# FFN down projection in seven products of 512x512 blocks held in PSUM, with the gated rows kept on chip

## The chip, the cores and the metric

The kernel runs on one core of a Trainium2 chip. The metric is the device time of one execution in microseconds (us), lower is better. Engines are named as in the profile: PE (TensorE, matmuls), PEld (its weight loads), DVE (VectorE), ACT (ScalarE), POOL (GpSimd), SP (SyncE, which here only issues transfers). A name with q (SPq, POOLq) is the queue through which an engine issues transfers.

## The reference

Two residual layers over 1024 positions of width 1024 in float32: layer 0 mixes with causal differential attention and pooling, layer 1 with sliding-window attention, and each ends with the same gated feed-forward block. The change is in that block's last product alone.

```python
D_MODEL, SEQ, D_FF, DEPTH = 1024, 1024, 2816, 2

def conv_glu_ffn(x, norm_g, w_up, conv_w, conv_b, w_down):
    h = rms_norm(x, norm_g) @ w_up                       # (S, 2*D_FF)
    hp = jnp.pad(h, ((0, 0), (CONV_W - 1, 0), (0, 0)))
    c = conv_b
    for j in range(CONV_W):
        c = c + conv_w[j] * hp[:, j:j + S]
    gate, up = jnp.split(c, 2, axis=-1)
    return x + (jax.nn.silu(gate) * up) @ w_down         # the down projection

for layer in range(DEPTH):
    x = mixer(layer, x)
    x = conv_glu_ffn(x, ...)
```

## The kernel before

Activations lie transposed, channels on the 128 partitions and positions along the free axis, so x is 8 tiles of 128x1024 and the gated result G of an FFN is NF = 22 row blocks of 128x1024. Every product is made in three matmuls: each operand is split into a high part (fp32r, written by ACT, L127) and a low part (the rest, L128, on DVE or POOL), and hi x hi, hi x lo and lo x hi are added up in a PSUM bank of 128x512 (`mm3`, L114).

The up pass (`ffn_up`, L310) makes G block by block. It already multiplies 512x512 blocks in seven products, with the sums of weight blocks made on DVE (L430) and parts of results saved from PSUM by ACT (`snap`, L456). Its last steps for block 21 are matmuls (L336), bank sums (L460), a convolution over time (ACT L343, DVE L344 and L346), the gate's SiLU (ACT L352), the gated product (DVE L356) and a write of the block to DRAM, to the tile `gd`.

The down pass (`ffn_down`, L511) reads G back. It goes over pairs of row blocks: `fetch` loads two blocks of w_down (SP, into `wr`) and two of G (POOL, L523, into `gr`; the first pair into `xg`), each 512 KB, and splits them at full width (1024 columns) on ACT and DVE. `contract` (L256) then goes over the 16 banks of the output (8 row blocks d, 2 halves h of the positions), makes 6 matmuls in each (L119) and adds the bank to the x tile on DVE (L268). So x in SBUF is read and written 16 times per pair, 11 pairs per pass. For layer 0 the last pair is left to `layer_c` (L1046), which runs its first half, starts the query projection (`project_qk`, matmuls L553) and weaves the second half with it. With the last addition for a block goes `after`: in layer 0 `feed` (L1121) makes the next norm's inputs (ACT L220, L224, DVE L221, L229, then `norm_stats`, PE transposes L236 and a DVE reduction L238), in layer 1 a store to the output (L1184).

Buffers are pools with a number of slots by tag: `ws` 8 (split operands), `wr` 2 (raw weights), `x` 8, `xg` 16 (the split inputs of a projection, 4 KB a partition each), `rbc` 1, and in the down pass `gr` 4 and `g` 8. PSUM has 8 banks in tags s (3), q (3) and d (2). The order on each engine is not the order of the code: a scheduler lays the instructions out by priority on a simulated time line, and `urgent(n)` lifts the priority of what is inside it. Each engine then runs its instructions in that fixed order; one that waits holds up all behind it on its engine, and so do the transfers of one queue.

Of the kernel before, what the change touches and what calls it, by code (L numbers as in the profile page):

```python
# [25 lines left out]
HALF = 512  # L26
NF = 22
# [28 lines left out]
LO_OUT = 0  # L56

# [7 lines left out]
class Trunk:  # L65
# [16 lines left out]
    DOWN = {"gr": 4, "g": 8}  # L82
# [428 lines left out]
    def ffn_down(self, layer, xs, gd, after, begin=lambda: None):  # L511
        nc, I = self.nc, self.I

        def fetch(i):
            ws, gs = [], []
            for k in range(2):
                for lst, tag, stage, src in (
                        (gs, "g", "gr", gd[(i + k) * P:(i + k + 1) * P, :]),
                        (ws, "ws", "wr", I["w_down"][layer, i + k])):
                    if i == 0 and lst is gs:  # L520
                        tag = stage = "xg"
                    raw = self.big(stage)
                    (nc.gpsimd if lst is gs else nc.sync).dma_start(raw[:], src)  # L523
                    hi, lo = self.big(tag, F32R), self.big(tag, F32R)
                    with self.urgent():
                        self.split(raw[:], hi[:], lo[:])
                    lst.append((hi, lo))
            return ws, gs
# [517 lines left out]
    def layer_c(self, w0, norm, before, xd, after):  # L1046
# [27 lines left out]
        x, sp = [], []  # L1074
# [58 lines left out]
    def run(self):  # L1133
# [38 lines left out]
        def begin():  # L1172
            self.norm_begin(2, False)
            w0.extend(self.in_weights(I["c_q"][0]))
# [99 lines left out]
```

## Time and profile before

| what | us |
|---|---|
| median of 3 runs (2156.82 to 2160.39) | 2159.76 |
| the profiled execution | 2160.71 |
| its span, first to last instruction | 2158.9 |
| PE busy in it | 2071.0 |
| DVE busy | 1609.1 |
| ACT busy | 1018.2 |
| POOL busy | 229.1 |
| DMA traffic, mean over the span | 86 GB/s |

The two down passes lie at about 846 to 1120 us and 1899 to 2156 us of the span; the up passes before them take about 410 to 869 and 1455 to 1915 us. Busy times of PE include the overlap of matmuls that follow each other; how far apart they start is read from the timeline. The mean granted clock of the run is 0.985 of full speed.

### The profile page before, as it was taken

What the parts mean: (1) busy time and instruction counts of PE and PEld (TensorE: products, weight loads), DVE (VectorE), ACT (ScalarE), POOL (GpSimd) and SP (SyncE); (2) the same over time, 40 slices, a digit from 0 to 9 for tenths busy, and PEclk for the clock granted to TensorE, in tenths of its full rate; (3) what the DMA queues carried; (4) which work ended last, traced back from release to release, by engine and by line L of the source; (5) the groups of instructions that cost most, each with busy time, mean ns of one, the idle gap of its engine ahead of it and who ended that gap; (6) DMA issues with size and microseconds to landing.
All of it is one profiled execution on the core that took longest, in us unless ns stands there. A gap on an engine that the chain in (4) does not pass through costs nothing.

```text
span 2158.9 us, 28587 instructions
## 1 busy us (share of the span) xinstructions
PE 2071.0 (96%) x10704; PEld 1767.5 (82%) x10704; DVE 1609.1 (75%) x2790; ACT 1018.2 (47%) x1895; POOL 229.1 (11%) x397
## 2 busy tenths in 40 slices
PE   8999999889999999899999999898999999989999
PEld 6999877677888888788899988776788888878887
DVE  6677777887777787766684887777877787776765
ACT  5476755454555555212155776553645445531210
POOL 1331542000000000100023230200000000010000
PEclk9999999999999999999999999999999999999999
DMA  4210221312222213522231111221222212262222
GB/s 167 88 50 21 79 89 57 109 34 94 78 88 88 84 73 104 213 104 86 71 127 42 48 40 40 79 79 40 97 78 88 88 71 86 88 240 82 88 89 78
DMA packets 59611, 186.03 MB, mean 86 GB/s; under 512 B 6864, under 2 KB 7376, under 8 KB 59472
## 3 DMA queue, kind: packets, MB, share of 16 engines
q1 hardware_dynamic: 43920, 140.16, 18.7%
q0 software_dynamic: 8640, 31.46, 4.1%
q10 hardware_dynamic: 6912, 12.59, 1.5%
q8 instruction: 84, 1.38, 0.3%
q14 instruction: 55, 0.45, 0.1%
HBM read 142.23 MB, written 41.94 MB: 85 GB/s over the span
## 4 chain that ended last, share of the span: by engine, by line
PE 87%; DVE 7%; ACT 4%; issue 1%; DMA 0%; POOL 0%; SPq 0%; DVEq 0%; ACTq 0%; POOLq 0%
PE pss L336 23%; PE psq L336 12%; PE psd L119 12%; PE psq L119 11%; PE pss L119 8%; PE psd L553 6%; PE psd L336 5%; PE pss L553 3%; PE psq L726 2%; PE pss L778 1%; PE pss L624 1%; PE pss L625 1%; PE psq L778 1%; DVE x L305 1%; DVE t L1014 1%
## 5 line engine op out<-in xcount | busy, mean ns | idle before, releaser
L336 PE MATMUL pss<-xg,ws 128*128 128x512 f32 x1248 | 298.8, 393 | 15.9 <-DVE xg L128 9.2
L336 PEld LDWEIGHTS pss<-xg,ws 128*128 128x128 f32 x1248 | 235.6, 189 | 68.5 <-DVE xg L128 10.1
L336 PE MATMUL pss<-T,ws 128*128 128x512 f32 x912 | 224.5, 389 | 3.4 <-ACT ws L127 3.4
L119 PE MATMUL psq<-g,ws 128*128 128x512 f32 x852 | 219.1, 391 | 2.5 <-ACT g L127 2.5
L336 PEld LDWEIGHTS pss<-T,ws 128*128 128x128 f32 x912 | 171.0, 188 | 39.7 <-ACT ws L127 4.2
L119 PEld LDWEIGHTS psq<-g,ws 128*128 128x128 f32 x852 | 160.2, 189 | 36.0 <-ACT g L127 3.0
L553 PE MATMUL psd<-ws,xg 128*128 128x256 f32 x1344 | 184.0, 284 | 2.2 <-DVE hms L562 1.7
L119 PE MATMUL psd<-xg,ws 128*128 128x512 f32 x624 | 168.0, 406 | 15.4 <-DVE x L268 14.6
L127 ACT ACTIVATE ws<-wr 128x512 fp32r<-128x512 f32 (+1 forms) x176 | 145.3, 829 | 72.4 <-PE pss L119 36.3
L127 ACT ACTIVATE g<-gr 128x1024 fp32r<-128x1024 f32 x40 | 42.0, 1051 | 290.4 <-PE pss L119 289.4
L119 PE MATMUL pss<-g,ws 128*128 128x512 f32 x684 | 176.2, 391 | 0.0
L553 PEld LDWEIGHTS psd<-ws,xg 128*128 128x128 f32 x1344 | 171.4, 191 | 4.8 <-DVE hms L562 2.5
L336 PE MATMUL psq<-xg,ws 128*128 128x512 f32 x696 | 169.5, 392 | 0.0
L128 DVE TENSOR_TENSOR ws<-hf,ws 128x512 fp32r<-128x512 f32 x152 | 104.0, 688 | 69.1 <-ACT ws L127 68.9
L336 PEld LDWEIGHTS psq<-xg,ws 128*128 128x128 f32 x696 | 131.9, 190 | 27.6
L268 DVE TENSOR_TENSOR x<-psq,x 128x512 f32<-128x512 f32 x160 | 109.6, 687 | 56.8 <-PE psq L119 56.5
L119 PEld LDWEIGHTS pss<-g,ws 128*128 128x128 f32 x684 | 129.3, 189 | 26.9
L119 PEld LDWEIGHTS psd<-xg,ws 128*128 128x128 f32 x624 | 115.1, 193 | 39.6 <-DVE x L268 17.1
L268 DVE TENSOR_TENSOR x<-psd,x 128x512 f32<-128x512 f32 x160 | 109.8, 687 | 47.0 <-PE psd L119 43.3
L128 DVE TENSOR_TENSOR ws<-wr,ws 128x512 fp32r<-128x512 f32 (+1 forms) x138 | 119.3, 865 | 20.6 <-ACT ws L127 20.6
L119 PE MATMUL psd<-g,ws 128*128 128x512 f32 x528 | 134.0, 389 | 0.0
L127 ACT ACTIVATE ws<-hf 128x512 fp32r<-128x512 f32 x152 | 94.9, 629 | 65.4 <-PE psq L336 27.2
(229 smaller groups left out, 3849.2 us busy)
## 6 DMA issues: line engine op xcount, KB each, us to landing
wr<-in_dram SPq DMA_DIRECT2D x130, 512.0 KB, 3.7
gd<-x SPq DMA_DIRECT2D x40, 512.0 KB, 2.6
gr<-gd POOLq DMA_DIRECT2D x40, 512.0 KB, 3.8
x<-in_dram SPq DMA_DIRECT2D x38, 512.0 KB, 4.5
xd<-x ACTq DMA_DIRECT2D x48, 256.0 KB, 2.1
x<-in_dram SPq DMA_DIRECT2D x32, 256.0 KB, 4.0
x<-xd POOLq DMA_DIRECT2D x16, 512.0 KB, 6.7
t<-in_dram SPq DMA_DIRECT2D x10, 512.0 KB, 3.6
```

The source lines that it names most:

```text
L119: self.nc.tensor.matmul(out, a, b, start=(k == 0), stop=(k == n - 1))
L127: nc.scalar.activation(hi, raw, AF.Copy)
L128: (eng or nc.vector).tensor_tensor(out=lo, in0=raw, in1=hi.bitcast(F32), op=ALU.subtract)
L268: nc.vector.tensor_tensor(out=xs, in0=po[:], in1=xs, op=ALU.add)
L305: nc.vector.scalar_tensor_tensor(out=xs, in0=xs, scalar=g, in1=self.nrbc[:, sl], op0=ALU.mult, op1=ALU.mult)
L336: nc.tensor.matmul(bank[:], a, b, start=start and k == 0, stop=k == n - 1, skip_group_check=open)
L553: self.nc.tensor.matmul(out, a, m[:, d % 4, :], start=(n == 0), stop=(n == 23))
L624: nc.tensor.matmul(out, q[:, qs], his[m][:, ks], start=True, stop=False)
L625: nc.tensor.matmul(out, q[rows, qs], lo[rows, ks], start=False, stop=True)
L726: nc.tensor.matmul(po[:, :256], tt[:, kb * P:(kb + 1) * P], v, start=(b == 0 and t == 0), stop=(b == j and t == 1))
L778: nc.tensor.matmul(pu[:], a, b, start=d + n == 0, stop=d == ND - 1 and n == 2)
L1014: nc.vector.tensor_scalar(pv[:, n, k0:2 * P], pv[:, n, k0:2 * P], rl[:, n:n + 1], None, ALU.mult)
```

## The change

`ffn_down` is written anew. The output is four blocks, C = [[C11, C12], [C21, C22]], of 512 channels by 512 positions, the weights four blocks by half of the 22 row blocks and half of the output channels, and G four blocks by half of the row blocks and half of the positions. Seven products of such blocks, instead of eight, give all four, with sums of weight blocks and of G blocks as operands. Each product goes over K = 11 steps; a step makes four banks of 3 matmuls (L610 in the new file), and the four banks stay in PSUM over the whole product, some over several: products 1, 6, 7 and 4 add up in one set of banks, 5 and 3 in another, 2 in a third. After each product its four banks are added to x (L632, 28 times per pass).

G is now loaded once, in halves of 512 columns (POOL queue), into 11 tiles `b` and 11 of the `xg` tiles and stays there; the sums of G blocks are made in place on DVE (L573). The weight sums of products 5, 6 and 3 are kept in 5 more `xg` tiles and the `rbc` tile. Weights come in halves of rows (SP), in tiles that hold two halves; where both belong to two steps, one transfer of 512 KB brings them, elsewhere two of 256 KB. `lead` prepares the operands of step n + 3 (AHEAD) and asks for the weights of step n + 9 (FETCH) at each step. The halves of the first four G blocks are loaded early into `hf` tiles (EARLY). Splits are at 512 columns.

In layer 0 the next norm is begun after product 3 and fed with the first half of the positions after products 3 and 7, with the second after 2 and 4; the first weights of the query projection are loaded after product 2, and `layer_c` runs product 4 whole before it starts that projection in the code.

```diff
@@ class Trunk
-    DOWN = {"gr": 4, "g": 8}
+    DOWN = {"b": 11, "r": 3}
@@ ffn_down
-        nxt = fetch(0)
-        x = [self.big("x") for _ in range(ND)]
-        for d in range(ND):
-            nc.gpsimd.dma_start(x[d][:], xs[d * P:(d + 1) * P, :])
-        for i in range(0, NF - 2, 2):
-            ws, gs = nxt
-            nxt = fetch(i + 2)
-            self.drain(self.contract(ws, [self.halves(g) for g in gs], x, banks="dqsdqsqs"))
-        ws, gs = nxt
-        begin()
-        return lambda h: self.contract(ws, [self.halves(g) for g in gs], x, after, "qd", (h,))
+        K = NF // 2
+        seq = [(p, k) for p in (1, 5, 6, 3, 7, 2, 4) for k in range(K)]
+        pairs = {1: (0, lo), 6: (0, lo), 3: (K, lo), 2: (K, lo), 4: (K, hi)}
+        stages = {p: ("r", "wr", "r", "wr", "r") for p in (5, 6, 3, 7, 2)}
+        stages[1], stages[4] = ("wr", "wr", "r", "r", "r"), ("r",)
...
+        b1 = [self.half() for _ in range(EARLY)]
+        for k in range(EARLY):
+            nc.gpsimd.dma_start(b1[k][:], g(k, hi))
+        bb = [self.big("b") for _ in range(K)]
+        cc = [self.big("xg") for _ in range(K)]
+        b11, b21 = [t[:, lo] for t in bb], [t[:, hi] for t in bb]
+        b12, b22 = [t[:, lo] for t in cc], [t[:, hi] for t in cc]
+        held = [self.big("xg") for _ in range(5)] + [self.big("rbc")]
+        sums = [held[k // 2][:, (k % 2) * HALF:(k % 2 + 1) * HALF] for k in range(K)]
...
+        def prepare(p, k):
+            r = raws.pop((p, k))
+            with self.urgent(9000):
+                if p == 1:
+                    l, m = r, b1[k][:] if k < EARLY else b11[k]
+                elif p == 5:
+                    l = combine(sums[k], r[0], r[1], ALU.add)
+                    m = combine(b11[k], b12[k], b11[k])
+                elif p == 6:
+                    l = combine(sums[k], sums[k], r)
+                    m = combine(b11[k], b22[k], b11[k])
+                elif p == 3:
+                    l, m = combine(sums[k], r, sums[k]), b22[k]
+                elif p == 7:
+                    l = combine(r[0], r[0], r[1])
+                    m = combine(b22[k], b22[k], b12[k])
+                elif p == 2:
+                    l, m = r, b21[k]
+                else:
+                    l, m = r, combine(b21[k], b21[k], b11[k])
+                ops[p, k] = operand(l), operand(m)
...
+        def product(p):
+            if p in (1, 5, 2):
+                banks[p] = [self.bank(t) for t in ("ssqd" if p == 1 else "sqqd")]
+            else:
+                banks[p] = banks[5] if p == 3 else banks[1]
+            n0 = seq.index((p, 0))
+            last = K - 2 if p == 4 else K
+            for k in range(last):
+                for m in range(4):
+                    multiply(p, k, m)
+                lead(n0 + k)
+            for m in range(4):
+                for k in range(last, K):
+                    multiply(p, k, m)
+            d0 = 4 if p in (5, 7, 4) else 0
+            cols = hi if p in (1, 2, 4) else lo
+            for m in range(4):
+                xm = x[d0 + m][:, cols]
+                with self.urgent(12000):
+                    nc.vector.tensor_tensor(out=xm, in0=banks[p][m][:], in1=xm, op=ALU.add)
...
+        for p in (1, 5, 6, 3):
+            product(p)
+        begin(0)
+        done(0, 0)
+        product(7)
+        done(4, 0)
+        after(None, 0, None)
+        product(2)
+        begin(1)
+        done(0, 1)
+        def rest():
+            product(4)
+            done(4, 1)
+            after(None, 1, None)
...
@@ layer_c
-        self.drain(before(0))
+        self.drain(rest)
         q0 = self.project_qk(w0, norm, qs[0], "s", "rbc")
-        ahead = before(1)
-        self.drain(islice(ahead, 4))
-        for _ in ahead:
-            next(q0)
```

Where instructions stand now is told by the built program's order, not by the code. Lines of the new file are 3 higher than before up to `ffn_up`: L336 is now L339, L460 is L463, L344, L346 and L356 are L347, L349 and L359, and the low part of a split, L128, is L131.

DVE at the end of layer 0's up pass, before: the last bank sums (L460), convolutions (L344, L346) and gated product (L356) of block 21 (x_1536 and x_1537), between splits of the down pass (L128) and its first additions of banks to x (L268).

```order
L460 TENSOR_TENSOR x_1535_8139<-snap_1534_8137,psq_1533_8112 128x512
L460 TENSOR_TENSOR x_1530_8076<-snap_1532_8110,psq_1533_8112 128x512
L128 TENSOR_TENSOR ws_1570_8243<-wr_1568_8240,ws_1569_8242 128x1024
L344 SCALAR_TENSOR_TENSOR x_1536_8154<-x_1535_8139,conv_1042_4996,x_1536_8154 128x1023
L344 SCALAR_TENSOR_TENSOR x_1537_8171<-x_1530_8076,conv_1042_4996,x_1537_8171 128x1023
L346 SCALAR_TENSOR_TENSOR x_1536_8154<-x_1535_8139,conv_1042_4996,x_1536_8154 128x1022
L346 SCALAR_TENSOR_TENSOR x_1537_8171<-x_1530_8076,conv_1042_4996,x_1537_8171 128x1022
L128 TENSOR_TENSOR g_1561_8225<-gr_1559_8222,g_1560_8224 128x1024
L268 TENSOR_TENSOR x_1551_8206<-psd_1571_8246,x_1551_8206 128x512
L268 TENSOR_TENSOR x_1551_8206<-psq_1572_8254,x_1551_8206 128x512
L356 TENSOR_TENSOR x_1536_8154<-x_1537_8171,x_1536_8154 128x1024
```

DVE at the same place now; ws_1597 and ws_1598 are the two operands of step 5 of product 1, from the weight tile r_1581 and the G tile b_1547.

```order
L463 TENSOR_TENSOR x_1535_8139<-snap_1534_8137,psq_1533_8112 128x512
L573 TENSOR_TENSOR xg_1565_8212<-wr_1602_8381 128x512
L347 SCALAR_TENSOR_TENSOR x_1536_8154<-x_1535_8139,conv_1042_4996,x_1536_8154 128x1023
L463 TENSOR_TENSOR x_1530_8076<-snap_1532_8110,psq_1533_8112 128x512
L349 SCALAR_TENSOR_TENSOR x_1536_8154<-x_1535_8139,conv_1042_4996,x_1536_8154 128x1022
L347 SCALAR_TENSOR_TENSOR x_1537_8171<-x_1530_8076,conv_1042_4996,x_1537_8171 128x1023
L349 SCALAR_TENSOR_TENSOR x_1537_8171<-x_1530_8076,conv_1042_4996,x_1537_8171 128x1022
L131 TENSOR_TENSOR ws_1597_8342<-r_1581_8282,ws_1597_8342 128x512
L359 TENSOR_TENSOR x_1536_8154<-x_1537_8171,x_1536_8154 128x1024
L131 TENSOR_TENSOR ws_1598_8345<-b_1547_8194,ws_1598_8345 128x512
```

The additions to x that stood here are gone, and an operand of the running product stands behind the gated product instead.

PE around the norm statistics of the first half in layer 0 (transposes into a bank of tag d), before: they stand between matmuls of the query projection (L553) and of the last pair.

```order
L553 MATMUL pss_1904_10052<-ws_1860_9767,xg_1851_9754 128x256
L553 MATMUL pss_1904_10052<-ws_1861_9768,xg_1851_9754 128x256
L553 MATMUL pss_1904_10052<-ws_1860_9767,xg_1852_9755 128x256
L236 MATMUL psd_1878_9882<-idn_122,hf_1863_9781 128x128 x4
L119 MATMUL psd_1889_9921<-g_1812_9592,ws_1815_9598 128x512
L119 MATMUL psd_1889_9921<-g_1813_9593,ws_1815_9598 128x512
```

PE around the same statistics now: the fourth step of product 2 (three banks), the transposes (L239), and then the fourth bank, psd_1785, of the first four steps.

```order
L610 MATMUL pss_1782_9593<-ws_1787_9612,ws_1786_9609 128x512 x2
L610 MATMUL psq_1783_9594<-ws_1787_9612,ws_1786_9609 128x512 x2
L610 MATMUL psq_1784_9595<-ws_1787_9612,ws_1786_9609 128x512 x2
L239 MATMUL psd_1773_9567<-idn_122,hf_1736_9288 128x128 x4
L610 MATMUL psd_1785_9596<-ws_1763_9498,ws_1762_9495 128x512 x3
L610 MATMUL psd_1785_9596<-ws_1765_9516,ws_1764_9513 128x512 x3
L610 MATMUL psd_1785_9596<-ws_1768_9536,ws_1767_9533 128x512 x3
L610 MATMUL psd_1785_9596<-ws_1787_9612,ws_1786_9609 128x512 x3
```

The statistics moved ahead by most of two products, out of the projection and into product 2.

## Rows read from the trace of the kernel before

**Rows 1.** From the page: engines' busy time; chain that ended last, by engine.

```profile
PE 2071.0 (96%) x10704; PEld 1767.5 (82%) x10704; DVE 1609.1 (75%) x2790; ACT 1018.2 (47%) x1895; POOL 229.1 (11%) x397
...
PE 87%; DVE 7%; ACT 4%; issue 1%; DMA 0%; POOL 0%; SPq 0%; DVEq 0%; ACTq 0%; POOLq 0%
```

**Rows 2.** Windows (length, busy per engine, PE clock, DMA share, GB/s): up, starts, steady.

```profile
567.00:594.00 27.00, 27.00 (x121) 22.36 (x120) 22.83 (x30) 13.88 (x20) 0.00 (x0) 1.00 0.16 59
864.00:891.00 27.00, 21.29 (x88) 17.17 (x87) 20.04 (x24) 10.66 (x11) 6.29 (x12) 0.87 0.91 335
918.00:945.00 27.00, 27.00 (x121) 22.36 (x120) 18.98 (x27) 3.91 (x4) 1.06 (x2) 1.00 0.36 123
1917.00:1944.00 27.00, 21.29 (x85) 17.09 (x84) 23.92 (x30) 7.51 (x8) 5.16 (x10) 0.87 0.86 311
```

**Rows 3.** Timeline of PE in the steady pass: start, length, group, count.

```profile
894.11 2.88 PE L119 MATMUL psd<-g,ws 128*128 128x512 f32 x12
896.83 1.52 PE L119 MATMUL psq<-g,ws 128*128 128x512 f32 x6
```

**Rows 4.** Timeline of PE at the first pass's start; in brackets the wait.

```profile
868.97 1.52 PE L119 MATMUL pss<-xg,ws 128*128 128x512 f32 x6
870.33 1.52 PE L119 MATMUL psq<-xg,ws 128*128 128x512 f32 x6
877.57 2.93 PE L119 MATMUL psd<-xg,ws 128*128 128x512 f32 x6 [5.71 <-DVE x L268]
```

**Rows 5.** Window of 5 us behind that wait, columns as in rows 2.

```profile
875.00:880.00 5.00, 2.44 (x6) 1.96 (x7) 5.00 (x7) 3.83 (x4) 2.05 (x4) 0.50 1.02 406
```

**Rows 6.** Timeline of PE at the second pass's start.

```profile
1923.86 2.93 PE L119 MATMUL psd<-xg,ws 128*128 128x512 f32 x6 [5.71 <-DVE x L268]
1926.59 2.45 PE L119 MATMUL psq<-xg,ws 128*128 128x512 f32 x6
```

**Rows 7.** Groups by line and form (busy us, mean ns, idle before): splits, SiLU.

```profile
L128 DVE TENSOR_TENSOR ws<-hf,ws 128x512 fp32r<-128x512 f32 x152 | 104.0, 688 | 69.1 <-ACT ws L127 68.9
...
L127 ACT ACTIVATE ws<-hf 128x512 fp32r<-128x512 f32 x152 | 94.9, 629 | 65.4 <-PE psq L336 27.2 <-ACT ws L127 23.6 <-DVE hf L430 9.0
...
L352 ACT ACTIVATE x<-x 128x1024 f32<-128x1024 f32 x40 | 42.5, 1062 | 46.0 <-DVE x L346 46.0
```

**Rows 8.** Timeline of DVE in the up pass, back to back.

```profile
707.13 0.69 DVE L128 TENSOR_TENSOR ws<-x,ws 128x512 fp32r<-128x512 f32 x1
707.73 0.69 DVE L430 TENSOR_TENSOR hf<-wr,x 128x512 f32<-128x512 f32 x1
```

**Rows 9.** Timeline of DVE at the first pass's start.

```profile
870.91 2.47 DVE L344 SCALAR_TENSOR_TENSOR x<-x,conv,x 128x1023 f32<-128x1023 f32 x2
873.30 2.47 DVE L346 SCALAR_TENSOR_TENSOR x<-x,conv,x 128x1022 f32<-128x1022 f32 x2
...
876.83 0.68 DVE L268 TENSOR_TENSOR x<-psd,x 128x512 f32<-128x512 f32 x1
...
878.02 1.22 DVE L356 TENSOR_TENSOR x<-x,x 128x1024 f32<-128x1024 f32 x1
```

**Rows 10.** Transfers: page's issues (us to landing), first 25 us, 846 to 900 us.

```profile
gr<-gd POOLq DMA_DIRECT2D x40, 512.0 KB, 3.8
...
DMA packets 3744, 7.53 MB, mean 301 GB/s; under 512 B 672, under 2 KB 928, under 8 KB 3744
...
x<-in_dram SPq DMA_DIRECT2D x16, 256.0 KB, 6.2
...
DMA packets 3603, 12.72 MB, mean 235 GB/s; under 512 B 400, under 2 KB 528, under 8 KB 3600
```

**Rows 11.** Timelines of POOL and of DVE where the projection's weights are split.

```profile
1120.82 5.21 POOL L128 TENSOR_TENSOR ws<-wr,ws 128x1024 fp32r<-128x1024 f32 x2 [16.38 <-ACT ws L127]
...
1119.54 0.68 DVE L229 TENSOR_TENSOR hf<-hf,hf 128x512 f32<-128x512 f32 x1
...
1121.37 5.21 DVE L229 TENSOR_TENSOR hf<-hf,hf 128x512 f32<-128x512 f32 x2
```

More of the change, by code (lines that the diff above doesn't have):

```diff
@@ L509, in ffn_up, with ffn_down, stage, fetch @@
                 raws[i + 2] = load(i + 2)
-    def ffn_down(self, layer, xs, gd, after, begin=lambda: None):
+    def ffn_down(self, layer, xs, gd, after, begin=lambda part: None):
         nc, I = self.nc, self.I
[L514 to L528, printed above, removed]
-        nxt = fetch(0)
-        x = [self.big("x") for _ in range(ND)]
+        w = I["w_down"][layer]
+        K = NF // 2
+        lo, hi = slice(0, HALF), slice(HALF, S)
+        HL = (P, 2, HALF)
+        seq = [(p, k) for p in (1, 5, 6, 3, 7, 2, 4) for k in range(K)]
+        pairs = {1: (0, lo), 6: (0, lo), 3: (K, lo), 2: (K, lo), 4: (K, hi)}
+        raws, ops = {}, {}
+        stages = {p: ("r", "wr", "r", "wr", "r") for p in (5, 6, 3, 7, 2)}
+        stages[1], stages[4] = ("wr", "wr", "r", "r", "r"), ("r",)
+        taken = dict.fromkeys(stages, 0)
+        def stage(p):
+            t = self.big(stages[p][taken[p] % len(stages[p])], F32, HL)
+            taken[p] += 1
+            return t
+        def fetch(p, k):
+            if p in pairs:
+                if k % 2 == 0:
+                    t, n = stage(p), min(2, K - k)
+                    off, cols = pairs[p]
+                    nc.sync.dma_start(
+                        t[:, :n, :], w[off + k:off + k + n, :, cols].rearrange("i p c -> p i c"))
+                    raws[p, k], raws[p, k + 1] = t[:, 0, :], t[:, 1, :]
+                return
+            t = stage(p)
+            first, second = ((k, hi), (K + k, hi)) if p == 5 else ((k, lo), (k, hi))
+            for n, (row, cols) in enumerate((first, second)):
+                nc.sync.dma_start(t[:, n, :], w[row, :, cols])
+            raws[p, k] = t[:, 0, :], t[:, 1, :]
+        g = lambda i, cols: gd[i * P:(i + 1) * P, cols]
+        b1 = [self.half() for _ in range(EARLY)]
[7 more added lines that the diff above has]
+        sums = [held[k // 2][:, (k % 2) * HALF:(k % 2 + 1) * HALF] for k in range(K)]
+        x = [self.big("x") for _ in range(ND)]
+        for k in range(EARLY, K):
+            nc.gpsimd.dma_start(b11[k], g(k, hi))
+        for k in range(K):
+            if k < EARLY:
+                nc.gpsimd.dma_start(b11[k], g(k, hi))
+            nc.gpsimd.dma_start(b12[k], g(k, lo))
@@ new lines, in ffn_down, with combine, operand @@
+        for k in range(K):
+            nc.gpsimd.dma_start(b21[k], g(K + k, hi))
+        def combine(out, a, b, op=ALU.subtract):
+            nc.vector.tensor_tensor(out=out, in0=a, in1=b, op=op)
+            return out
+        def operand(src):
+            op = self.big("ws", F32R, HL)
+            self.split2(src, op)
+            return op
+        def prepare(p, k):
[19 more added lines that the diff above has]
+                ops[p, k] = operand(l), operand(m)
@@ new lines, in ffn_down, with multiply @@
+        banks = {}
+        def multiply(p, k, m):
+            a, b = ops[p, k]
+            opens, closes = p in (1, 5, 2) and k == 0, p in (3, 2, 4) and k == K - 1
+            ah, al = (a[:, t, m * P:(m + 1) * P] for t in range(2))
+            for n, (l, r) in enumerate(((ah, b[:, 0, :]), (ah, b[:, 1, :]), (al, b[:, 0, :]))):
+                nc.tensor.matmul(banks[p][m][:], l, r, start=opens and n == 0, stop=closes and n == 2,
+                                 skip_group_check=p != 2)
+        def product(p):
[18 more added lines that the diff above has]
+                    nc.vector.tensor_tensor(out=xm, in0=banks[p][m][:], in1=xm, op=ALU.add)
@@ new lines, in done, with lead @@
+        def done(d0, h):
+            for d in range(d0, d0 + 4):
+                after(d, h, x[d][:, h * HALF:(h + 1) * HALF])
+        def lead(n):
+            if n + FETCH < len(seq):
+                fetch(*seq[n + FETCH])
+            if n + AHEAD < len(seq):
+                prepare(*seq[n + AHEAD])
+        for n in range(FETCH):
+            fetch(*seq[n])
+        for n in range(AHEAD):
+            prepare(*seq[n])
+        for p in (1, 5, 6, 3):
+            product(p)
+        begin(0)
```

26 lines of the change are left out of this document (17 added, 9 removed).

## The prediction

> **What bounds the kernel now.** I read the busy totals first, then the chain that ended last, then the windows over the two down passes, then the timelines of the places where the passes begin and end. TensorE is busy for 2071.0 us of a span of 2158.9 us, and 87% of the chain is TensorE; VectorE stands on it with 7% [rows 1]. In the steady part of a down pass TensorE is busy in all of a 27 us window at granted clock 1.00, while VectorE is busy for 19.0 us, ScalarE for 3.9 and the DMA engines for 0.36 of it [rows 2]. So a matmul that goes there is worth its whole interval. That interval is not the 389 ns which the profile gives one matmul: twelve start between 894.11 and 896.83 us, thus 2.72/12 = 0.2267 us each [rows 3]. Only the start of the pass shows a hole: TensorE waits 5.71 us for VectorE to empty a bank, and the matmuls behind the hole run slowly [rows 4], at a granted clock of 0.50 of full speed over 875 to 880 us, the 1.2 GHz level, for part of them [rows 5]. The second layer has the same hole [rows 6].
>
> **What goes.** Each pass now has 11 pairs x 16 banks x 6 = 1056 matmuls of 512 columns; after, 7 products x 11 steps x 4 banks x 3 = 924. That is 132 fewer per pass and 264 in all: 264 x 0.2267 = **59.8 us** off the path. Also gone are 11 x 16 = 176 bank additions per pass, of which 28 stay, and 44 splits of 1024 columns.
>
> **What comes, on VectorE.** Each product step splits two operands of 512 columns (154 subtractions per pass), and 88 additions or subtractions form the block sums. With the 28 bank additions that is 270 operations of 512 columns, against 176 + 88 halves = 264 before: the total hardly moves, its place does. The profile gives one 0.69 us [rows 7], but back to back they start 0.60 us apart [rows 8]; 270 x 0.60 = 162 us lies beside 924 x 0.2267 = 209.5 us of TensorE. The sums are not even: counted in the new order from one product's bank additions to the next, VectorE has 43 operations (25.8 us) up to the end of product 5, 53 (31.8) for product 6 and 37 (22.2) for product 3, each against 132 x 0.2267 = 29.9 us. Only product 6 is over, by 1.9 us. Operands are made three steps (8.2 us) ahead, so this may cost nothing; I take the whole excess, 2 x 1.9 = **3.8 us**, with bounds 0 and, at 0.687 us per operation, 2 x 6.5 = 13 us. ScalarE makes 154 copies of 0.63 us per pass [rows 7], some 97 of 209 us, and is no limit.
>
> **What moves at the start of a pass.** Call E the end of the last up matmul. Before, 12 matmuls are left behind E (2.9 us), and TensorE restarts at E + 8.6 us, when VectorE is through the last gate's work [rows 4, 9]. After, the order shows four steps of product 1 woven in ahead of E and two matmuls behind it; step 5 needs a split that stands behind the same gate work. Up to it VectorE must do: one bank sum 0.6, three convolution passes of 1.2 [rows 9], one weight split 0.6, the wait for the gate's activation (1.1, rows 7), the gate product 1.1, the split 0.6, together 7.6 us. Its data is the sixth load on the POOL queue behind a tile that comes free 2.7 us before E, and six loads of 0.26 MB take 4.7 us at the 335 GB/s of the busiest window [rows 2], and one load of 0.52 MB lands 3.8 us after its issue, 1.6 of them at that rate, so some 2.2 us come on top [rows 10]: E + 4 to 6 with SP's loads beside them, about when VectorE is through. TensorE idles some 7.3 us instead of 5.7, and the slow matmuls behind it stay: 2 x 1.6 = **3.2 us** lost, with bounds of a gain of 11.4 (both holes gone) and a loss of 12.
>
> **What the first layer adds.** The norm of the first half of the sequence needs a bank of tag d for its transposes, and product 2 wants the same bank; in the new order the first four steps of product 2 do three banks (36 matmuls, 8.2 us) and leave the fourth until the statistics are read. VectorE reaches that point 18 operations (10.8 us) after the first bank of product 7 is done, which is 2.0 us before that product ends, and four transposes and a reduction of 512 columns, taken as two operations more, add some 1.3 us: 10.1 against 8.2. One operand chain (0.63 + 0.69 us, rows 7) follows before the next step: together **3 us**, bounds 0 and 8. In product 4 the projection weights of the next layer hold four of the eight operand buffers, so operands are only two steps ahead, and POOL splits four weight tiles beside it. In the trace of before two such POOL operations take 5.21 us, and a VectorE addition with two SBUF inputs, 0.68 us before it, then shows 5.21 us for two [rows 11]. There it hides behind projection matmuls; now it stands before operands. Four times 2.4 us is 9.6; 48 projection matmuls fill part, so I take **3 us**, bounds 0 and 9.6. The end of the kernel keeps its form: last bank, one addition, one store.
>
> **Transfers.** The weights come as 99 half rows of 0.26 MB per pass instead of 22 of 0.52 MB: 26 MB for 11.5, mostly in loads of half the size. The gated rows are loaded once, as 48 halves. From 3 us before E to the end of product 5, some 63 us, POOL has 11.5 MB queued and SP 9.4 MB: 20.9 MB, or 332 GB/s. The densest 27 us of before moved 335 GB/s, and the first 25 us of the kernel, with 16 loads of 256 KB in flight, 301 GB/s [rows 2, 10]. So it just fits, and what is late lies first on the x tiles, which VectorE can wait for with its three steps in hand. I book nothing, and price it as a rival. The Trainium skill ("DMA: Bandwidth & Descriptors", section Bandwidth) asks for loads of 1 MiB for three quarters of peak and gives each a fixed 2 us. By its fit an estimate for one 0.26 MB load is 2.6 us, and one load at a time would make the weights 99 x 2.6 = 257 us, longer than the pass. The 301 GB/s above speak against that wherever many loads are queued, as here.
>
> **The sum.** The profiled execution took 2160.7 us (0.95 above the median shown): 2160.7 - 59.8 + 3.8 + 3.2 + 3 + 3 = 2113.9, thus **2114 us**.
>
> **The rivals.** (a) VectorE bounds the products: every operation at its full 0.687 us (13 in place of 3.8), product 4 blocked by POOL throughout (9.6 in place of 3), the statistics at 8 and the starts with 12. That is 2114 + 9.2 + 6.6 + 5 + 8.8 = 2144 with all of them, and 2126 to 2139 with some. For it: operands, sums and bank additions share one in-order engine, and an early bank addition makes all behind it wait. Against: in the up pass VectorE has a like load, 22.8 of 27 us, with TensorE at 27.0 of 27 [rows 2]. (b) Transfers bound the start: the 20.9 MB land at the 235 GB/s that 846 to 900 us show [rows 10], in 89 us instead of 63, 26 us late per pass: 2114 + 52 = 2166, **slower**. It decides from 20.9/(63 + 23.4) = 242 GB/s downwards. Against it: those 54 us were not asking for more all the time. (c) All the waits hide and only the matmuls count: 2100.9, and a little under it if a hole shrinks. (d) The change doesn't save the matmuls: the order shows 1848 matmuls in the two passes, so no.
>
> **How the numbers follow.** My forecast with its own terms, 2106 to 2125: 0.58. Rival (a), 2125 to 2150: 0.22. (c), below 2106: 0.13. (b): 0.07, of which 0.05 ends above 2164, the rest between. The range for 8 in 10 reaches from 2100 to 2139: it takes in (c) almost whole and (a) up to the sum of three of its four bounds. What a measurement here can tell from no change is about 0.2%, some 4 us. Faster than that 0.93, within it 0.02, slower 0.05.
>
> **What will show it.** The matmul intervals inside a product should read 2.72 us for twelve at granted clock 1.00; a product that takes more than 30 us names its wait. Right would be: a hole of 6 to 9 us behind E with VectorE or a load as its end, VectorE near 26 of 27 us in product 6, a pause of 2 to 5 us in product 2 of the first layer alone, and the second layer shorter than the first by about that. Wrong would be waits of TensorE at every step in products 5 to 7 (VectorE, rival a), or VectorE waiting for weight tiles there (rival b), or a granted clock that stays low within a product.

## The result and the profile after

The changed kernel takes 2133.82 us (median of 4 runs, 2131.87 to 2135.76), against 2159.29 us for the kernel before beside it: ratio 0.9884, 95% interval 0.9867 to 0.9901. That is faster by 25.5 us. The forecast was 2114, faster by 46; the range of 2100 to 2139 holds the time. So the sign was right, and 20 us of the expected gain are missing: the time lies outside the 2106 to 2125 us of the forecast's own terms, and inside the range because that was drawn wide enough for most of rival (a). The profiled execution took 2133.47 us (span 2131.5), against 2160.71 for the one of before: 27.2 us to account for.

From the page of the changed kernel, busy time by engine:

```profile
PE 2017.4 (95%) x10440; PEld 1718.2 (81%) x10440; DVE 1611.6 (76%) x2890; ACT 1107.7 (52%) x2115; POOL 257.9 (12%) x449
```

Against [rows 1], whose columns these are, there are exactly 264 matmuls fewer (10704 to 10440), and VectorE's busy time has not moved (1609.1 to 1611.6). TensorE's busy time fell by 53.6 us while the span fell by 27.4: about half of what was saved has come back as waiting. The windows say where. First pass, in columns as in [rows 2]: the start, behind it, the change from product 5 to product 6, product 6 and 3, product 2, and product 4.

```profile
862.00:889.50 27.50, 15.94 (x64) 12.75 (x63) 14.86 (x20) 9.57 (x14) 13.29 (x25) 0.81 0.81 298
889.50:917.00 27.50, 27.50 (x121) 22.16 (x120) 24.05 (x41) 10.49 (x18) 5.90 (x11) 1.00 1.03 391
917.00:944.00 27.00, 21.58 (x87) 17.14 (x86) 25.97 (x44) 8.80 (x17) 0.00 (x0) 0.87 0.57 188
944.00:971.00 27.00, 27.00 (x120) 22.34 (x119) 23.19 (x39) 11.52 (x20) 0.00 (x0) 1.00 0.39 127
...
1025.00:1052.00 27.00, 24.98 (x104) 20.02 (x103) 24.24 (x49) 13.86 (x25) 0.00 (x0) 0.94 0.31 107
1052.00:1079.00 27.00, 26.47 (x124) 21.90 (x123) 21.72 (x29) 14.86 (x25) 5.35 (x3) 1.00 0.41 137
```

A window of 27 us holds 120 matmuls of 512 columns when nothing waits. The start holds 64, the third window 87, the one of product 2 104; the others are full or nearly so. In the third one VectorE is busy for 25.97 of 27 us: the "near 26" of the forecast, but with TensorE standing beside it.

TensorE's timeline at these places (start, length, group, count, in brackets the wait). First pass: start, product 6, statistics; then the second pass: last up matmuls, start, product 6, end.

```profile
870.03 0.61 PE L610 MATMUL psd<-ws,ws 128*128 128x512 f32 x2
882.21 1.22 PE L610 MATMUL pss<-ws,ws 128*128 128x512 f32 x2 [11.56 <-ACT ws L130]
...
887.58 1.07 PE L610 MATMUL pss<-ws,ws 128*128 128x512 f32 x4
...
933.01 0.61 PE L610 MATMUL psd<-ws,ws 128*128 128x512 f32 x2
934.89 0.73 PE L610 MATMUL pss<-ws,ws 128*128 128x512 f32 x2 [1.27 <-ACT ws L130]
...
940.24 2.08 PE L610 MATMUL pss<-ws,ws 128*128 128x512 f32 x4 [4.15 <-DVE ws L131]
...
943.78 0.63 PE L610 MATMUL pss<-ws,ws 128*128 128x512 f32 x2
...
1038.10 1.07 PE L610 MATMUL psq<-ws,ws 128*128 128x512 f32 x4
1040.41 0.66 PE L239 MATMUL psd<-idn,hf 128*128 128x128 f32 x4 [1.24 <-DVE hf L232]
1041.84 4.61 PE L610 MATMUL psd<-ws,ws 128*128 128x512 f32 x12 [0.78 <-DVE ms L241]
1046.29 0.40 PE L610 MATMUL pss<-ws,ws 128*128 128x512 f32 x1
...
1903.53 2.88 PE L339 MATMUL psq<-xg,ws 128*128 128x512 f32 x12
...
1918.90 1.22 PE L610 MATMUL pss<-ws,ws 128*128 128x512 f32 x2 [12.04 <-ACT ws L130]
...
1975.94 2.07 PE L610 MATMUL pss<-ws,ws 128*128 128x512 f32 x4 [4.14 <-DVE ws L131]
...
2125.93 1.52 PE L610 MATMUL psd<-ws,ws 128*128 128x512 f32 x6
```

What a place costs is the time between two of its rows less the matmuls between them at 0.2267 us. The second pass as a whole: 878 of its 924 matmuls stand behind E = 1903.53 + 2.72 = 1906.25; they are worth 199.0 us. The last six begin at 2125.93 and take 1.36 us, so the pass ends at 2127.29, 221.0 us behind E: 22.0 us are lost. Of before, these are E and the end of the second pass:

```profile
1912.55 2.88 PE L336 MATMUL psq<-xg,ws 128*128 128x512 f32 x12
...
2151.96 2.88 PE L119 MATMUL psd<-g,ws 128*128 128x512 f32 x12
```

There 1020 matmuls (231.2 us) take 2154.68 - 1915.27 = 239.4 us: 8.2 lost. The same arithmetic by place, with the slow matmuls behind each wait in it: 18 matmuls lie between 870.03 (E of the first pass) and 887.58 us, where full speed is back, and 17.55 - 4.08 = 13.5 us are lost at the first start; 14 between 933.01 and 943.78, so 10.77 - 3.17 = 7.6 at product 6; 16 and four transposes of 0.09 us between 1038.10 and 1046.29, so 8.19 - 3.99 = 4.2 at the statistics. In the second pass it is 14.4 at the start and 7.6 at product 6, together its 22.0. Before, the starts lost 7.4 us (the wait and the slow matmuls of [rows 4]) and the 8.2 just worked out.

| place | forecast, us | measured, us |
|---|---|---|
| matmuls saved | -59.8 | -59.8 |
| starts of the passes | 3.2 | (13.5 - 7.4) + (14.4 - 8.2) = 12.3 |
| product 6 (VectorE's excess) | 3.8 | 7.6 + 7.6 = 15.2 |
| statistics in product 2 | 3 | 4.2 |
| product 4 beside POOL | 3 | 0.5 |
| sum | -46.8 | -27.6 (execution: -27.2) |

The sum closes to 0.4 us. Two terms, 9.1 and 11.4 us too small, make up what is missing, and they are the two that hang on the order of VectorE's work and of SP's queue.

### The profile page after: what moved, and what is told of

It reads as the page before. It is cut to its first block, busy times and chain, and to the rows that moved or that the text cites. A ratio compares the mean times of both kernels' runs of the same rounds, so it can differ in the third digit from the quotient of the medians.

```text
span 2131.5 us, 28465 instructions
## 1 busy us (share of the span) xinstructions
PE 2017.4 (95%) x10440; PEld 1718.2 (81%) x10440; DVE 1611.6 (76%) x2890; ACT 1107.7 (52%) x2115; POOL 257.9 (12%) x449
## 4 chain that ended last, share of the span: by engine, by line
PE 83%; DVE 8%; ACT 4%; issue 2%; DMA 2%; POOL 1%; SPq 0%; ACTq 0%; DVEq 0%; POOLq 0%
PE pss L339 22%; PE psq L339 12%; PE pss L610 8%; PE psq L610 6%; PE psd L679 6%; PE psd L122 6%; PE psd L610 5%; PE psd L339 4%; PE pss L679 3%; PE psq L122 3%; PE psq L852 1%; PE pss L904 1%; PE pss L750 1%; PE pss L751 1%; DMA r<-in_dram 1%
## 5 line engine op out<-in xcount | busy, mean ns | idle before, releaser
L339 PE MATMUL pss<-xg,ws 128*128 128x512 f32 x1248 | 298.6, 392 | 16.9 <-DVE xg L131 9.2
L339 PEld LDWEIGHTS pss<-xg,ws 128*128 128x128 f32 x1248 | 235.5, 189 | 69.4 <-DVE xg L131 10.0
L610 PE MATMUL pss<-ws,ws 128*128 128x512 f32 x726 | 204.3, 398 | 34.1 <-ACT ws L130 25.3
L339 PE MATMUL pss<-T,ws 128*128 128x512 f32 x912 | 224.5, 389 | 3.4 <-ACT ws L130 3.4
L339 PEld LDWEIGHTS pss<-T,ws 128*128 128x128 f32 x912 | 171.1, 188 | 39.6 <-ACT ws L130 4.3
L610 PEld LDWEIGHTS pss<-ws,ws 128*128 128x128 f32 x726 | 138.4, 192 | 66.1 <-ACT ws L130 26.9
L610 PE MATMUL psq<-ws,ws 128*128 128x512 f32 x660 | 185.3, 392 | 0.0
L339 PE MATMUL psq<-xg,ws 128*128 128x512 f32 x696 | 169.5, 392 | 0.0
L131 DVE TENSOR_TENSOR ws<-hf,ws 128x512 fp32r<-128x512 f32 x160 | 109.6, 689 | 73.3 <-ACT ws L130 73.1
L122 PE MATMUL psd<-xg,ws 128*128 128x512 f32 x576 | 152.4, 402 | 3.7 <-DVE x L271 2.8
L339 PEld LDWEIGHTS psq<-xg,ws 128*128 128x128 f32 x696 | 131.9, 190 | 27.6
L130 ACT ACTIVATE ws<-wr 128x512 fp32r<-128x512 f32 (+1 forms) x158 | 115.5, 735 | 72.3 <-PE pss L339 33.4
L610 PEld LDWEIGHTS psq<-ws,ws 128*128 128x128 f32 x660 | 125.3, 190 | 26.4
L610 PE MATMUL psd<-ws,ws 128*128 128x512 f32 x462 | 140.2, 397 | 0.8 <-DVE ms L241 0.8
L131 POOL TENSOR_TENSOR ws<-wr,ws 128x1024 fp32r<-128x1024 f32 x38 | 95.0, 2508 | 287.7 <-ACT ws L130 247.0
L347 DVE SCALAR_TENSOR_TENSOR x<-x,conv,x 128x1023 f32<-128x1023 f32 x80 | 102.6, 1282 | 30.0 <-ACT x L346 29.8
L130 ACT ACTIVATE ws<-xg 128x512 fp32r<-128x512 f32 x104 | 63.0, 624 | 109.1 <-PE psd L610 74.1
```

The source lines that it names most:

```text
L122: self.nc.tensor.matmul(out, a, b, start=(k == 0), stop=(k == n - 1))
L130: nc.scalar.activation(hi, raw, AF.Copy)
L131: (eng or nc.vector).tensor_tensor(out=lo, in0=raw, in1=hi.bitcast(F32), op=ALU.subtract)
L339: nc.tensor.matmul(bank[:], a, b, start=start and k == 0, stop=k == n - 1, skip_group_check=open)
L347: nc.vector.scalar_tensor_tensor(out=c[:, 1:], in0=hr[:, :S - 1], scalar=cw(1), in1=c[:, 1:], op0=ALU.mult, op1=ALU.add)
L610: nc.tensor.matmul(banks[p][m][:], l, r, start=opens and n == 0, stop=closes and n == 2, skip_group_check=p != 2)
```

## The experiments

Each kernel is the changed one with the edit shown; each time was taken beside runs of the kernel before, so ratios are compared: 0.9884 is the changed kernel. Where one trace is laid beside another, times are counted from E, since the up passes do not end at the same moment. One per mille is 2.2 us.

**First weights of product 6 first.** Where product 6 begins, VectorE does this (after; L573 are block sums, L131 splits, L632 bank additions):

```profile
928.67 1.29 DVE L573 TENSOR_TENSOR xg<-xg,wr 128x512 f32<-128x512 f32 x2
...
931.08 1.29 DVE L573 TENSOR_TENSOR xg<-xg,wr 128x512 f32<-128x512 f32 x2
...
932.89 1.29 DVE L573 TENSOR_TENSOR xg<-xg,r 128x512 f32<-128x512 f32 x2
934.09 0.69 DVE L632 TENSOR_TENSOR x<-pss,x 128x512 f32<-128x512 f32 x1
934.69 1.29 DVE L573 TENSOR_TENSOR xg<-xg,r 128x512 f32<-128x512 f32 x2
935.89 1.28 DVE L632 TENSOR_TENSOR x<-psq,x 128x512 f32<-128x512 f32 x2
937.09 0.68 DVE L632 TENSOR_TENSOR x<-psd,x 128x512 f32<-128x512 f32 x1
937.69 0.68 DVE L131 TENSOR_TENSOR ws<-xg,ws 128x512 fp32r<-128x512 f32 x1
938.29 1.29 DVE L573 TENSOR_TENSOR xg<-xg,r 128x512 f32<-128x512 f32 x2
939.49 0.69 DVE L131 TENSOR_TENSOR ws<-b,ws 128x512 fp32r<-128x512 f32 x1
```

By the order of the instructions these sums belong to steps 3 and 4, 7 and 8, then 1 and 2 (932.89), 5 and 6, and 9 and 10. The first split of step 1 starts at 937.69, behind all but the last of them and behind four bank additions, and TensorE restarts at 940.24, when its second split is done. The reason is on SP's queue: the weights of steps 3, 4, 7 and 8 go to the two wr tiles, which fall free first, and are asked for first (at 914.75 us; those of steps 1 and 2 at 920.17).

```diff
+        stages[6] = ("wr", "wr", "r", "r", "r", "r")
```

> The changed kernel with one line more: the weights of product 6's first four steps come in the two wr tiles, which fall free first, so that the loads and with them VectorE's sums for its first steps are asked for first; the number of operations on every engine is the same. Order theory (the pause before product 6 comes from the order of VectorE's work: the sum for the first step of product 6 stands behind the sums for its steps 3, 4, 7 and 8): the 1.3 + 4.2 us of idle TensorE near 935 and 940 us and the 0.4 + 4.1 us of the second layer go, and the slow matmuls behind them: some 8 us per pass, 2133.8 to about 2118. Volume theory (VectorE has too much to do there, in whatever order): a pause of 4 us or more stays at the change from product 5 to 6 or moves into product 6, time above 2129.

Measured 2120.67 us, ratio 0.9833 (0.9817 to 0.985): 11 us less by ratio, 14.6 by the profiled spans (2116.9). TensorE's timeline at product 6, first and second pass:

```profile
942.30 1.20 PE L611 MATMUL pss<-ws,ws 128*128 128x512 f32 x4 [1.18 <-DVE ws L131]
...
1971.95 1.20 PE L611 MATMUL pss<-ws,ws 128*128 128x512 f32 x4 [0.31 <-DVE ws L131]
```

The window over it in the first pass:

```profile
916.00:943.00 27.00, 25.82 (x114) 21.07 (x113) 25.97 (x44) 12.24 (x22) 0.00 (x0) 1.00 0.55 180
```

VectorE has 44 operations and 25.97 us in this window, as in the one of the changed kernel, and TensorE gets 114 matmuls through in place of 87. So it is the order; the excess of work that the forecast counted costs no more than the 1.18 and 0.31 us that are left.

**Loads held back.** The loads that product 1 does not need were put behind a copy of one column from its last G tile.

```diff
+        def gated(out, row):
+            nc.gpsimd.tensor_copy(out=out[:, 0:1], in_=b11[GATE][:, 0:1])
+            nc.gpsimd.dma_start(out, row)
```

> The changed kernel with the loads of G and x that product 1 does not need held back until the last G tile of product 1 has landed (a copy of one column on POOL ahead of each). Transfer theory (the hole behind the up pass is 11.6 and 12.0 us long because the weight tile of step 5 lands 10 us after its issue, among some twenty other loads): that tile lands in 4 to 6 us, the hole shrinks to about 7.5 us in both layers, 2 x 4 = 8 us less from this place. VectorE theory (the gate's work of the last block sets the hole): it stays at 11 us or more. The order of the weight loads also shifts in this kernel, so that the loads for product 6 come first step first; by the order theory the pause before product 6 goes too, another 16 us: about 2110. If product 5 now waits for its G tiles, a new pause stands near 895 to 905 us.

Measured 2154.05 us, ratio 0.9978 (0.9966 to 0.9989): almost all of the gain gone. The first hole did shrink, to 6.31 and 6.29 us, but then products 5, 6 and 3 wait, longest for 9.47 us in product 5 of the first pass and for 4.45 and 6.21 us in that of the second. TensorE's timeline, first pass:

```profile
919.91 0.79 PE L615 MATMUL pss<-ws,ws 128*128 128x512 f32 x1 [9.47 <-ACT ws L131]
```

VectorE's in front of this wait:

```profile
917.84 0.69 DVE L578 TENSOR_TENSOR xg<-r 128x512 f32<-128x512 f32 x1 [3.26 <-DMA r<-in_dram]
```

It is the last of seven waits for a weight tile of product 5, of 1.95 to 3.26 us each, between 890 and 920 us. The loads held back now run beside these weight loads, and the DMA engines move 394 GB/s from 905 to 925 us. As a test of the first hole the run is not clean: the order on SP's and POOL's queues moved too. The weight tile of step 5 was issued 9.7 us ahead of E (864.29; E is 873.95 here) in place of 0.9 us (869.09; E is 870.03), and the last seven G tiles of product 1 from 12.0 us ahead in place of 1.7. The weight tile landed no sooner after its issue, 10.9 us, where 4 to 6 were expected. The run on SP's queue below tests the issue by itself.

**Statistics behind product 2.**

```diff
         done(4, 0)
-        after(None, 0, None)
         product(2)
+        after(None, 0, None)
```

> The changed kernel with the statistics of the first half of the norm behind product 2 in place of ahead of it. Bank theory: product 2 of layer 0 takes its fourth bank at once, the idle 1.2 + 0.8 us, the transposes' gap and the slow matmuls near 1040 us go, 4.5 us less: 2129.3. Rival: the statistics are late for the projection, which then waits as long: 2133.8 within 1.5 us. Layer 1 and the other pauses stay as they are.

Measured 2126.39 us, ratio 0.9859 (0.9844 to 0.9873): 5.4 us less by ratio. TensorE has no wait in products 2 and 4 of layer 0 any more. The bank was the cause. The profiled spans differ by 6.1 us; the 4.2 and 0.5 us of the table and a wait of 0.39 us in the second pass make 5.1 of them, and the last 1 us is not accounted for.

**Weights of steps 5 and 6 early.**

```diff
-        stages[1], stages[4] = ("wr", "wr", "r", "r", "r"), ("r",)
+        stages[1], stages[4] = ("wr", "wr", "rbc", "r", "r"), ("r",)
```

> The changed kernel with the weights of steps 5 and 6 of product 1 in the rbc tile, which is free during the up pass, so that they are loaded before the up pass ends; the G tile of step 5 still comes at its old place. Transfer theory: ScalarE no longer waits for weights at 880 us, only for the G tile; the hole shrinks by 2 to 4 us per layer, 2126 to 2130. VectorE theory: the hole stays at 11 us or more, 2133.8 within 1.5 us.

Measured 2129.55 us (2124.51 to 2133.43), ratio 0.9873 (0.9851 to 0.9894), which cannot be told from the changed kernel's 0.9884. Two executions took 2124.5 and 2125.9 us, two 2133.2 and 2133.4, and the profile is of the first. So the median lies where it was expected, but the reading rests on the rows. The first hole fell to 6.29 and 6.40 us, further than expected, but a second one followed, of 6.27 and 9.17 us. TensorE's timeline, first pass:

```profile
876.12 1.22 PE L610 MATMUL pss<-ws,ws 128*128 128x512 f32 x2 [6.29 <-ACT ws L130]
...
888.95 2.07 PE L610 MATMUL pss<-ws,ws 128*128 128x512 f32 x4 [6.27 <-DVE ws L131]
```

VectorE's in front of the second hole:

```profile
886.40 0.69 DVE L573 TENSOR_TENSOR xg<-r 128x512 f32<-128x512 f32 x1 [8.39 <-DMA r<-in_dram]
```

VectorE waits 8.39 us for a weight tile of product 5, to make a block sum that only a later product needs, and the splits of product 1, whose data has arrived, stand behind that wait.

**VectorE in the order of the steps.** The same number of operations, loads and buffers; an edge of issue order keeps what belongs to a step behind the splits of the step two before it.

```diff
+            n = len(done_at)
+            order = self.tc.issue_after(done_at[n - LAG].ins) if n >= LAG else nullcontext()
-            with self.urgent(9000):
+            with self.urgent(9000), order:
...
+            done_at.append(last[0])
```

> The changed kernel with VectorE held to the order of the steps: block sums and splits of a step are issued behind the splits of the step two before it; loads, counts and buffers stay. Order theory: the pause before product 6 (1.3 + 4.2 and 0.4 + 4.1 us, with slow matmuls some 8 us per pass) goes though VectorE has the same number of operations; the hole behind the up pass stays at 11 to 12 us, since the late weight tile sets it. 2133.8 - 14 = about 2120. Volume theory: a pause of 4 us or more stays near 935 us, and holding VectorE back costs more besides: 2134 or above.

Measured 2110.4 us, ratio 0.9773 (0.9756 to 0.9791): 24 us less by ratio, more than expected. TensorE's waits in the first pass up to the end of product 7 (the second has 6.29 and 1.73 us there):

```profile
878.71 1.22 PE L618 MATMUL pss<-ws,ws 128*128 128x512 f32 x2 [6.29 <-ACT ws L579]
912.23 0.80 PE L618 MATMUL pss<-ws,ws 128*128 128x512 f32 x1 [3.34 <-ACT ws L579]
```

The pause before product 6 is gone, as the order theory says. The 3.34 us in product 5 are new: VectorE waits 3.54 us there for a weight tile. The first hole fell as well, against my expectation: it was on VectorE's order too, by way of SP's queue. This is the chain in the changed kernel, first on VectorE:

```profile
867.51 0.69 DVE L573 TENSOR_TENSOR xg<-wr 128x512 f32<-128x512 f32 x1 [6.39 <-PE pss L339]
```

Then on SP's queue:

```profile
868.24 0.81 SPq L545 DMA_DIRECT2D wr<-in_dram  x2
869.09 3.35 SPq L538 DMA_DIRECT2D r<-in_dram  x3
```

And on ScalarE:

```profile
880.06 0.63 ACT L130 ACTIVATE ws<-r 128x512 fp32r<-128x512 f32 x1 [7.48 <-DMA r<-in_dram]
```

A block sum for step 2 of product 5 (867.51) stands on VectorE among the last work of the up pass. It writes to an `xg` tile that held an operand of the up pass, and waits 6.39 us until TensorE is through with that tile. Only when the sum has read its wr tile can SP load the next weights of product 5 into that tile (868.24), and the weights of step 5 of product 1 stand behind that load (869.09). They land 11.0 us later, among the other loads, and ScalarE waits for them until 880.06. With the steps in order the load for step 5 is issued at 862.15, 9.7 us ahead of E (871.80 there).

**SP's queue alone.** The weight loads of product 5 behind those of product 1; VectorE's order ahead of product 6 left as it was.

```diff
+            with self.tc.issue_after(first[0]):
+                for n, (row, cols) in enumerate(rows):
+                    nc.sync.dma_start(t[:, n, :], w[row, :, cols])
```

> The changed kernel with one order changed on SP's queue: the weight loads of product 5 are issued behind those of product 1. VectorE's order ahead of product 6 stays as it was (the sums for steps 3, 4, 7 and 8 ahead of the one for step 1). Queue theory (the first hole is long because the weight tile of step 5 stands on SP's queue behind a load for product 5 that waits for a buffer which VectorE frees late): the tile is issued 7 us earlier, the hole falls from 11.6 and 12.0 to about 6.3 us in both layers; the pause of 5.4 us before product 6 stays. 2133.8 - 11 = about 2123, more if VectorE waits for product 5's weights with splits of product 1 behind it. Rival (the transfers alone, whatever the queue's order): the hole stays at 10 us or more.

Measured 2138.75 us, ratio 0.992 (0.9905 to 0.9934): slower than the changed kernel, though the first hole is 6.29 us in both passes. SP's issue of the weights of step 5, first pass:

```profile
860.76 0.39 SPq L538 DMA_DIRECT2D r<-in_dram  x1
```

TensorE's waits in the same pass:

```profile
877.32 1.22 PE L613 MATMUL pss<-ws,ws 128*128 128x512 f32 x2 [6.29 <-ACT ws L130]
889.10 2.07 PE L613 MATMUL pss<-ws,ws 128*128 128x512 f32 x4 [5.37 <-DVE ws L131]
941.32 2.08 PE L613 MATMUL pss<-ws,ws 128*128 128x512 f32 x4 [3.92 <-DVE ws L131]
```

VectorE in front of the second of them:

```profile
887.75 0.69 DVE L576 TENSOR_TENSOR xg<-wr 128x512 f32<-128x512 f32 x1 [7.94 <-DMA wr<-in_dram]
```

The tile was issued at 860.76, again 9.7 us ahead of E (870.42), landed 5.8 us later, and the hole is the one of VectorE's and ScalarE's work on the gate: the queue theory holds. But the loads of product 5 now arrive later, and VectorE waits 7.94 us for one, with splits of product 1 behind it, as in the run with early weights. The pause before product 6 stays at 3.92 us, as its order does. So a repair of the queue alone only moves the wait.

**Repairs together, and a stricter order.** First the new weights for product 6 with the late statistics; then these two with the early weights and the order of the steps; then the same with the order held one step apart (LAG = 1).

> Product 6's first weights in the wr tiles and the statistics behind product 2 together. If the two costs are independent, the gains seen apart (14.6 and 6.1 us in the profiled executions) add up: a profiled execution near 2113 and a median of 2112 to 2116. If one pause only moves to the other place: 2117 or more.

> The two repairs of the run beside it, the weights of steps 5 and 6 in the rbc tile, and VectorE held to the order of the steps. Theory: with the weights early the first hole falls to 6.3 us, the time of the last block's gate on VectorE, as in the run with early weights alone; the second hole there (6.3 and 9.2 us) was VectorE waiting for a weight tile of product 5 while splits of product 1 stood behind that wait, and goes when the sums stand in step order. One hole of 6.3 us per pass with its slow matmuls (8 us) is left: some 5 us per pass less than with two repairs, 2102 to 2107. Rival: transfers are late for product 1 itself, the second hole stays at 4 us or more wherever VectorE's order puts it: 2112 or more.

> The version with four repairs, but VectorE held to the order one step apart in place of two, so that no block sum is made ahead while a split waits for ScalarE. VectorE is busy for 26.5 of 27 us in product 6 with two steps. If it has no time to lose there, the waits for ScalarE that this puts into each step (some 0.5 us of the 2.7) make TensorE wait in products 5, 6 and 3: 2108 to 2130. If the operands in hand hide it: 2103.5 within 2 us.

Two repairs: 2114.26 us, ratio 0.9787 (0.9772 to 0.9801). The profiled span is 2111.4 us, 20.1 less than that of the changed kernel, against 14.6 and 6.1 for the two apart, so the gains add up. Four repairs: 2103.5 us (2103.28 to 2104.02), ratio **0.9738** (0.9722 to 0.9755), faster than both kernels. Of TensorE's waits in the passes the one at each start is left, here the first pass's, and one of 0.34 us in product 4:

```profile
875.32 1.22 PE L619 MATMUL pss<-ws,ws 128*128 128x512 f32 x2 [6.29 <-ACT ws L580]
```

The window over product 6 is full:

```profile
916.00:943.00 27.00, 27.00 (x121) 22.35 (x120) 26.46 (x44) 12.84 (x23) 0.00 (x0) 1.00 0.40 127
```

VectorE works 26.46 of 27 us there and TensorE all of them. The stricter order: 2117.19 us, ratio 0.9823 (0.9807 to 0.984), 13.7 us slower than with two steps by the medians and 18 by ratio, with waits of 0.3 to 1.7 us in products 6, 3, 7 and 4 and this window over product 6:

```profile
916.00:943.00 27.00, 26.15 (x114) 20.71 (x113) 23.04 (x38) 9.38 (x17) 0.00 (x0) 1.00 0.34 109
```

VectorE gets 38 operations done in place of 44. It waits for ScalarE 7 times there, 2.5 us in all, and once for TensorE (2.3 us), against one wait of 0.8 us with two steps. So VectorE has next to no slack in product 6, but in a good order it is enough.

## Why the prediction was right and wrong

**What bounds, and the matmuls saved: right.** 264 matmuls are gone, and away from the three waits twelve of them take 2.72 us at granted clock 1.00 (the window of 944 to 971 us).

**The starts: 3.2 us forecast, 12.3 measured.** The step that failed is the landing of the data at "E + 4 to 6". I worked it out for the G tile on POOL's queue alone, and took "SP's loads beside them" as covered. The G tile did come at E + 5 (issued at 868.38, it landed 6.6 us later). The weight tile came at E + 10 (E is 870.03, its split starts at 880.06). The quoted piece of the new order even shows the cause, the block sum of xg_1565 from wr_1602 in its second row among the up pass's last work, but I gave that row no price, neither its own time nor that of what is queued behind it: the buffer that it frees, the load that waits for this buffer, and the load behind that one on SP. The part on VectorE was sound: 7.3 us forecast, and 6.3 to 6.4 us in each of the six runs in which the weights came in time. In the version with four repairs a start loses 9.1 us (18 matmuls from 868.41 to 881.57 us), so the two lose 1.7 + 0.9 = 2.6 us more than before, near the 3.2 forecast.

**Product 6: 3.8 us forecast, 15.2 measured.** I counted operations between two products' bank additions and found an excess of 1.9 us per pass. That count was sound: in the right order no more than 1.18 and 0.31 us are left of the pause, and VectorE fills 26.46 of 27 us. What failed is "operands are made three steps ahead". An engine that runs its instructions in a fixed order is ahead only if the next operand is the next thing it does. Here the sums of later steps and four bank additions came first; with the loads asked for in another order, or VectorE held to the steps, they did not.

**A wait costs more than its length.** I gave slow matmuls to the starts only. Behind the 4.15 us of product 6 the clock is granted at half of full speed too, the 1.2 GHz level, and for part of the time behind the statistics (windows of the changed kernel, columns as in [rows 2]):

```profile
940.50:943.00 2.50, 2.50 (x7) 1.95 (x8) 2.50 (x5) 0.00 (x0) 0.00 (x0) 0.50 0.64 216
...
1042.00:1045.00 3.00, 3.00 (x9) 2.39 (x10) 2.54 (x12) 2.05 (x4) 0.00 (x0) 0.62 0.00 0
```

At product 6, 5.42 us of waiting became 7.6 us lost in the first pass, and 4.53 us became 7.6 in the second. The wait of 1.18 us that was left there in the first experiment cost little beyond itself: its next four matmuls took 1.20 us. At the statistics it went both ways at the same waits: the twelve matmuls behind them took 4.61 us here and 4.60 in the first experiment, but 3.02 to 3.06 in the runs with held-back loads, with early weights and on SP's queue alone. What decides it is open.

**Statistics: 3 us forecast, 4.2 measured,** 5.4 by the run without the conflict; the mechanism was as described, the slow matmuls were missing. **Product 4: 3 us forecast, 0.5 measured.** POOL's splits do slow VectorE. POOL's timeline at the start of product 4:

```profile
1066.77 2.79 POOL L131 TENSOR_TENSOR ws<-wr,ws 128x1024 fp32r<-128x1024 f32 x1 [75.01 <-ACT ws L130]
```

VectorE's at the same time:

```profile
1067.80 2.31 DVE L224 SCALAR_TENSOR_TENSOR xg<-x,par,xg 128x512 fp32r<-128x512 f32 x1
```

The same operation took 0.75 us just before, at 1066.54. An addition (L232) beside the second split took 2.89 us. But these are operations for the norm, in a stretch in which VectorE is busy for 21.7 of 27 us, and TensorE waits only 0.53 us in it (26.47 of 27 us busy). **The second pass is shorter than the first** by what the first layer adds, as forecast: 13.5 + 7.6 + 4.2 + 0.5 = 25.8 us are lost in the first and 22.0 in the second.

**The rivals.** (a) had the right size, 2126 to 2144, and half of the right mechanism. The starts at 12 us were its bound; but VectorE's operations start 0.60 us apart at product 6 (937.09 and 937.69), not 0.687, and POOL does not matter. "An early bank addition makes all behind it wait" was near the truth, and I left it in a sentence where it needed a price. (b) was the wrong fear in size: the chip moved 391 GB/s in the window behind the start, far above the 242 from which it decides, and the run with four repairs has no wait of TensorE there at 385 GB/s (889 to 916 us). That is also the answer to the rule of the Trainium skill ("DMA: Bandwidth & Descriptors", section Bandwidth) weighed ahead: with loads of 256 and 512 KB and many in flight, the trace does not show the loss that the rule gives to small loads. The fixed 2 us that the prediction takes from the Trainium skill stands on the same page under "Anatomy of one DMA", for loads that GpSimd issues; the weights here are issued by SP. Rival (b) is not empty, though: in four of the experiments VectorE waits 3 to 8 us at a time for a weight tile of product 5. (c), 2100.9, is near what the change can do: the version with four repairs comes to 2103.5, with the hole of 6.3 us left in each pass.

Not settled: what makes a single load slow at the start of a pass. The tile of step 5 took 11.0 us to land when it was issued 0.9 us ahead of E. Issued 9.7 us ahead, it took 5.8 us in the run on SP's queue alone and 6.1 in the one with the steps in order, but 10.9 with the later loads held back; TensorE's wait was 6.3 us in all three. So the earlier issue is enough to mend the hole. Whether a quicker landing would be too was not tested; by an estimate from these numbers it would, since 5.8 us from the late issue is E + 4.9, about when the G tile came.

## What to carry to other kernels

Counting an engine's operations per stage tells whether there is room; it does not tell whether the next thing that is needed is the next thing done. Where an in-order engine makes operands for several stages, read the order around each change of stage, and price every instruction for later work by what stands behind it: on its own engine, through the buffer that it frees, and on the queue whose load waits for that buffer. Where a scheduler fills gaps with early work, hold this work behind the running stage by a few steps: here that alone took the changed kernel from 2133.8 to 2110.4 us with two steps between, while one step, beside the other repairs, lost 14 us again (2117.2 against 2103.5).

## What was not expected of the hardware

The DMA engines moved 391 GB/s over 27.5 us at a busy share of 1.03, against 335 in the densest window of [rows 2]. At that load a 512 KB weight tile landed 11.0 us after its issue, against 5.8 us for the same tile issued 8.7 us sooner before E. And the clock fell to half after waits that look short. Behind a single wait of 4.14 us (second pass of the run with late statistics, 1969.5 to 1973 us) it was granted at 0.50. Two waits of 2.0 us together left it at 0.62 over 3 us behind them in the changed kernel, and at 1.00 in the run with early weights (1036 to 1040 us). Here 5.4 us of waiting cost 7.6, and the 2.0 us cost 4.2.
